# Grouped convolution: semaphores cleared by GpSimd while stores are in flight, store counters taken back by the sync engine's last waits

## The chip, the cores and the metric

One core of one Trainium2 chip. The metric is device time in microseconds (us) of one execution, median over the runs named. "Span" is the stretch that the profile covers, from the first to the last instruction record; the reported time is about 1.7 us longer. SP is the sync engine, which here issues the stores; POOL is GpSimd. Start times and semaphore counts given to a hundredth are from the trace's records.

## The reference

A 3x3 convolution, padded by one, in 8 groups: 16 images of 64 channels of 64x64, 128 output channels, float32 in and out.

```python
for g in range(groups):
    for b in range(batch):
        for co in range(c_out_per_group):
            for ci in range(c_in_per_group):
                for kh in range(k):
                    for kw in range(k):
                        output[b, g * c_out_per_group + co] += \
                            weight[g * c_out_per_group + co, ci, kh, kw] * \
                            x_pad[b, g * c_in_per_group + ci, kh:kh+h, kw:kw+w]
```

## The kernel before

The input is loaded by GpSimd with a cast to bf16, TensorE runs the nine taps as small matmuls, VectorE and ScalarE copy the results from PSUM into 16 output buffers, and SP stores each buffer twice: 32 stores of 1 MiB. Each buffer has its own counter, `st0` to `st15`; a store adds 16 to it when it has landed, so each ends at 32. A small class keeps one counter per engine and drops waits that were already made.

```python
class Order:
    ...
    def wait(self, *needs):
        best = {}
        for need in needs:
            if need is not None:
                sem, val = need
                best[sem.num] = max(best.get(sem.num, (0, sem))[0], val), sem
        for num, (val, sem) in best.items():
            if self.seen.get(num, 0) < val:
                self.eng.wait_ge(sem, val)
                self.seen[num] = val

    def done(self, ins):
        ins.then_inc(self.sem, 1)
        self.n += 1
        return self.sem, self.n
...
    def sem(name):
        s = nc.alloc_semaphore(name)
        sems.append(s)            # everything in sems is cleared at the end
        return s
...
    stored = [sem(f"st{i}") for i in range(NOB)]
...                               # in finish(), once per store
                    SP.wait(*self.wrote[im])
                    nc.sync.dma_start(outf[img][:, s0 : s0 + HALF], ob[slot]).then_inc(stored[slot], 16)
                    uses[slot] += 1
...                               # the end of the program
    SP.wait(*((stored[s], 16 * uses[s]) for s in range(NOB)))
    POOL.wait(SP.done(nc.sync.nop()))
    nc.clear_and_free_semaphores(sems)
```

The compiler packs the 16 last waits into eight SP instructions of two waits each, and puts the signal to GpSimd onto the last of them. Behind this program the tile framework closes the block: all five engines exchange signals, GpSimd clears the framework's own six semaphores, and all are released twice.

## Time and profile before

| | before |
|---|---|
| reported time, median of 6 runs | 130.13 us (129.95 to 130.27) |
| span of the profiled run | 128.2 us |
| last matmul ends | 93.5 us |
| last count of the last store (st15) | 126.81 us |
| from there to the last record (the "tail") | 1.38 us |
| from there to the end of the reported time | 3.09 us |

What bounds the kernel is read in the prediction below. Two more lines of the page of the kernel before, DMA queues with their packets, MB and share of 16 engines, are needed later: queue 1 carries the stores, queue 14 fetches of instructions.

```profile
q1 hardware_dynamic: 4752, 33.59, 62.9%
...
q14 instruction: 2, 0.02, 0.0%
```

From st6 to st15 a store lands every 2.449 us (nine gaps, 22.04 us together before). One MiB in 2.449 us is 428 GB/s, the rate that the view by stretches shows.

### The profile page before, as it was taken

How to read it: one execution, taken by the hardware profiler on the slowest of the kernel's cores; microseconds unless marked ns; L12 is line 12 of the kernel's file. 1: busy time of each engine (PE TensorE's matmuls, PEld its weight loads, DVE VectorE, ACT ScalarE, POOL GpSimd, SP SyncE). 2: the span in 40 equal slices, each digit the busy share in tenths (PEclk: the TensorE clock that was granted, in tenths of full speed). 3: DMA queues.
4: the chain of work that ended last, by engine and by line, in shares of the span. 5: the costliest groups of instructions: out<-in, count | busy, mean ns of one | idle time of the engine just before them, and what ended most of it. 6: DMA issues, size and time to landing. Idle time of an engine off the chain costs nothing.

```text
span 128.2 us, 3808 instructions
## 1 busy us (share of the span) xinstructions
PE 86.9 (68%) x2322; PEld 41.2 (32%) x1170; DVE 45.8 (36%) x74; ACT 37.0 (29%) x68; POOL 7.2 (6%) x19
## 2 busy tenths in 40 slices
PE   0199999999999999999999999999910000000000
PEld 0153353544435355444553544544500000000000
DVE  1840465446444645446544564465440000000000
ACT  4030354345333543336333453354330000000000
POOL 5960000000000000000000000000000000000000
PEclk9999999999999999999999999999996555555555
DMA  2999999999999999999999999999999999999950
GB/s 24 162 202 215 224 212 220 215 289 284 281 289 281 284 271 297 297 401 424 419 424 424 396 435 406 435 414 429 417 424 429 424 432 422 429 427 432 427 243 10
DMA packets 6271, 42.21 MB, mean 329 GB/s; under 512 B 848, under 2 KB 848, under 8 KB 1424
## 3 DMA queue, kind: packets, MB, share of 16 engines
q1 hardware_dynamic: 4752, 33.59, 62.9%
q0 software_dynamic: 1504, 8.39, 32.8%
q8 instruction: 13, 0.21, 0.6%
q14 instruction: 2, 0.02, 0.0%
HBM read 16.81 MB, written 33.55 MB: 393 GB/s over the span
## 4 chain that ended last, share of the span: by engine, by line
PE 67%; DVE 4%; issue 2%; POOL 1%; POOLq 0%; DVEq 0%; SPq 0%
PE bank L227 65%; DVE E L149 2%; DVE ob L254 2%; PE bank L162 2%; POOL ident L128 0%; POOL mask L123 0%; POOL mask L133 0%; POOL xn L106 0%; POOLq L123 0%; POOLq L316 0%; DVEq L75 0%; SPq L53 0%
## 5 line engine op out<-in xcount | busy, mean ns | idle before, releaser
L227 PE MATMUL bank<-xs,wS 32*64 32x504 bf16 (+3 forms) x1152 | 71.6, 374 | 0.6 <-issue 0.4
L227 PE MATMUL bank<-xn,wN 32*64 32x504 bf16 (+3 forms) x1152 | 71.8, 380 | 0.2 <-DVE ob L254 0.2
L254 DVE COPY ob<-bank 128x512 f32<-128x512 f32 x64 | 41.3, 686 | 45.4 <-PE bank L227 45.4
L254 ACT COPY ob<-bank 128x512 f32<-128x512 f32 x64 | 34.5, 589 | 51.2 <-PE bank L227 51.1
L222 PEld LDWEIGHTS <-wS 32*64 32x64 bf16 x576 | 27.5, 104 | 20.8 <-issue 9.9
L222 PEld LDWEIGHTS <-wN 32*64 32x64 bf16 x576 | 19.1, 106 | 25.0 <-issue 20.9
L162 PE MATMUL bank<-ident,E 128*128 128x128 bf16 x18 | 2.1, 313 | 5.9 <-DVE E L149 5.9
L106 POOL DMA_DIRECT2D xs<-in_x_dram x7 | 3.8, 543 | 0.0
L162 PEld LDWEIGHTS bank<-ident,E 128*128 128x128 bf16 x18 | 1.8, 148 | 5.9 <-DVE E L149 5.9
L149 DVE TENSOR_TENSOR E<-w_sb,mask 128x288 bf16<-128x288 f32 x5 | 2.9, 642 | 1.7 <-DMA w_sb<-in_weight_dram 1.7
L106 POOL DMA_DIRECT2D xn<-in_x_dram x5 | 2.9, 583 | 1.0 <-SPq L53 1.0
L172 ACT CAST wS<-bank 128x512 bf16<-128x512 f32 (+1 forms) x3 | 1.2, 487 | 5.2 <-PE bank L162 5.2
L172 DVE CAST wN<-bank 128x512 bf16<-128x512 f32 (+1 forms) x3 | 1.5, 551 | 0.7 <-PE bank L162 0.7
L172 ACT ACT_TABLE_LOAD x1 | 1.3, 1283 | 1.0 <-SPq L53 1.0
L117 DVE MEMSET mask<- 128x8 f32 x1 | 0.1, 65 | 1.1 <-SPq L53 1.1
L128 POOL TENSOR_SCALAR_AFFINE_SELECT ident<-ident 128x128 bf16<-128x128 bf16 x1 | 0.3, 306 | 0.0
L123 POOL TENSOR_SCALAR_AFFINE_SELECT mask<-mask 128x8 f32<-128x8 f32 x1 | 0.2, 211 | 0.1
L133 POOL TENSOR_SCALAR_AFFINE_SELECT mask<-mask 128x8 f32<-128x8 f32 x1 | 0.2, 199 | 0.0
L302 POOL MEMSET const-float32-0.0<- 128x1 f32 x1 | 0.1, 99 | 0.3 <-issue 0.3
L118 DVE MEMSET ident<- 128x64 uint32 x1 | 0.1, 112 | 0.0
L302 POOL MEMSET const-bfloat16-1.0<- 128x1 bf16 x1 | 0.1, 102 | 0.0
L302 POOL MEMSET const-uint8-127<- 128x1 uint8 x1 | 0.1, 102 | 0.0
(1 smaller groups left out, 0.1 us busy)
## 6 DMA issues: line engine op xcount, KB each, us to landing
out_dram<-ob SPq DMA_DIRECT2D x32, 1024.0 KB, 28.0
xn<-in_x_dram POOLq DMA_DIRECT2D x3, 1024.0 KB, 29.6
xs<-in_x_dram POOLq DMA_DIRECT2D x2, 1024.0 KB, 29.6
xn<-in_x_dram POOLq DMA_DIRECT2D x2, 512.0 KB, 7.6
xs<-in_x_dram POOLq DMA_DIRECT2D x2, 512.0 KB, 9.4
xs<-in_x_dram POOLq DMA_DIRECT2D x1, 768.0 KB, 48.4
xs<-in_x_dram POOLq DMA_DIRECT2D x2, 128.0 KB, 9.5
w_sb<-in_weight_dram SPq DMA_DIRECT2D x1, 36.0 KB, 1.8
```

The costliest lines, as they stand in the source:

```text
L106: nc.gpsimd.dma_start(t.rearrange("p h w -> p (h w)")[p0:p1, h0 * W : h1 * W], xr[row0 + p0 : row0 + p1, h0 * W : h1 * W],).then_inc(s, 16)
L117: m1 = DVE.done(nc.vector.memset(mask, 1.0))
L123: m3 = POOL.done(nc.gpsimd.affine_select(out=mask, in_=mask, compare_op=ALU.is_ge, fill=0.0, base=0, channel_multiplier=1, pattern=[[-COg, ...
L128: m4 = POOL.done(nc.gpsimd.affine_select(out=ident, in_=ident, compare_op=ALU.not_equal, fill=1.0, base=0, channel_multiplier=1, pattern=[ ...
L133: m5 = POOL.done(nc.gpsimd.affine_select(out=mask, in_=mask, compare_op=ALU.is_ge, fill=0.0, base=COg - 1, channel_multiplier=-1, pattern= ...
L149: e = DVE.done(nc.vector.tensor_mul(E[:, :, 32 * r : 32 * r + 32].rearrange("p t (g c) -> p t g c", c=CIg), wv.unsqueeze(2).to_broadcast([ ...
L162: ins = nc.tensor.matmul(banks[b][:, 128 * t : 128 * t + 128], E[:, t0 + t, off : off + 128], ident, start=True, stop=True,)
L172: free[b] = eng.done(copy(dst, banks[b][:, 0 : 128 * n]))
L222: pe.ldweights(w_ap, **pos)
L227: ins = pe.add_instruction(mybir.InstMatmult(name=nc.get_next_instruction_name(), engine=mybir.EngineType.PE, start_tensor_calc=k == 0, st ...
L254: free[b] = eng.done(copy(ob[slot][:, o0 : o0 + 512], banks[b]))
L302: nc = _bacc.Bacc("TRN2", target_bir_lowering=False, num_devices=1)
```

## The change

Its intent is to take GpSimd's clear out of the tail. A semaphore may be cleared only when nobody will count on it any more. For all but the store counters that is so when SP has issued its last store, near 100 us. The store counters are therefore left out of GpSimd's list, and each is taken back to zero by the wait that waits for it: "wait until at least 32, then subtract 32".

```diff
-    stored = [sem(f"st{i}") for i in range(NOB)]
+    stored = [nc.alloc_semaphore(f"st{i}") for i in range(NOB)]
...
-    SP.wait(*((stored[s], 16 * uses[s]) for s in range(NOB)))
+
     POOL.wait(SP.done(nc.sync.nop()))
     nc.clear_and_free_semaphores(sems)
+
+    for n in range(nob[0], nob[0] + NOB):
+        s = stored[n % NOB]
+        num = dict(sync_type="semaphore", id=s.num, ant_name=s.name)
+        nc.sync.add_instruction(mybir.InstEventSemaphore(
+            name=nc.get_next_instruction_name(), engine=mybir.EngineType.SP,
+            sync_info=mybir.SyncInfo(
+                on_wait=[mybir.SyncWait(wait_mode="sem-ge-imm", wait_value=16 * uses[n % NOB], **num)],
+                on_update=[mybir.SyncUpdate(update_mode="sem-sub-imm", update_value=16 * uses[n % NOB], **num)],
+            ),
+        ))
```

## The prediction

> **What bounds the kernel now.** I read the page first, for which engine or stage sets the end.
>
> ```profile
> span 128.2 us, 3808 instructions
> PE 86.9 (68%) x2322; PEld 41.2 (32%) x1170; DVE 45.8 (36%) x74; ACT 37.0 (29%) x68; POOL 7.2 (6%) x19
> ...
> PE   0199999999999999999999999999910000000000
> ...
> DMA  2999999999999999999999999999999999999950
> ```
>
> The matrix engine is full for three quarters of the span and idle in the last quarter, while the DMA row stays at 9 until the last two slices. So the last third is a drain of stores. The page's chain of work does not show this: it ends with an eviction at 94.7 us, because it follows engines and not transfers. I therefore asked for busy time by stretches (columns: stretch, length, busy time of each engine, clock, DMA share, GB/s).
>
> ```profile
> 95.00:122.00 27.00, 0.00 (x0) 0.00 (x0) 0.00 (x0) 0.00 (x0) 0.00 (x0) 0.53 1.01 428
> 122.00:126.85 4.85, 0.00 (x0) 0.00 (x0) 0.00 (x0) 0.00 (x0) 0.00 (x0) 0.50 0.35 147
> 126.85:128.20 1.35, 0.00 (x0) 0.00 (x0) 0.00 (x0) 0.00 (x0) 0.00 (x0) 0.50 0.00 0
> ```
>
> For 27 us nothing runs but stores, at 428 GB/s with all DMA engines taken; then the last store trickles out; then 1.35 us pass in which nothing moves at all. The change can touch only those 1.35 us. What fills them stands in the sync engine's waits after 99 us (waiter, releaser, us in total, times, longest):
>
> ```profile
> SPq L75 <- DMA out_dram<-ob: 26.3, 7, 11.9
> SPq L316 <- PEq L316: 0.5, 2, 0.3
> SPq L53 <- POOLq L53: 0.2, 1, 0.2
> ```
>
> and in the view by source line of L285, the clearing call, and of L53, where the tile framework closes the block (operation, count, ns min/median/max, first and last start):
>
> ```profile
> L285 POOLq DRAIN  x1: 116/116/116, 126.9 to 126.9; - x1
> L285 POOLq EVENT_SEMAPHORE_RANGE_CLEAR  x1: 224/224/224, 127.1 to 127.1; - x1
> ...
> L53 SPq NOP  x2: 13/13/13, 0.8 to 127.4; - x2
> ...
> L53 POOLq DRAIN  x1: 40/40/40, 127.4 to 127.4; - x1
> ```
>
> The reader is to see an ordered tail: the last store counted, then GpSimd's drain and clear, then the closing exchange of all five engines, in which the sync engine waits 0.2 us for GpSimd. Start times from the trace's records, in us: the counter of the last store (st15) is full at 126.81; SP passes the wait for it at 126.826, its last wait (st0 and st1, full long before), which also signals GpSimd, at 126.885; GpSimd drain 126.938, clear 127.083, its closing drain 127.356; SP no-op that has waited for that drain 127.422; two SP drains 127.489 and 127.553; GpSimd gathers at 127.585; a second clear and two rounds of release follow, the last record ending at 128.19.
>
> **What the Trainium skill says.** "Perfetto Trace Analysis", section "Sequencer-only Instruction (DRAIN, etc)": the record of such an instruction covers its execution alone; the wait before it and the spreading of its semaphore update after it lie outside. The trace agrees: the waits last 28 ns in the records but follow each other in 59 ns, so I count start to start, not durations. "DMA: Bandwidth & Descriptors", section "Why a DMA increments its semaphore by 16 and not by 1": each of the DMA's engines adds 1 when its own share is written, and only the full 16 means that all has landed. Here st15 gets 15 of its last 16 counts between 122.82 and 125.44 us and the last at 126.81, so one engine is 1.4 us behind, and both kernels must wait for it. "Runtime: NRT & Kernel Launch", section "The ~15µs preamble/postamble breakdown": user semaphores are also zeroed around each launch. The trace shows every semaphore updated once more at 129.0 to 129.28 us, behind the span; the change does not touch that.
>
> **The change part by part.**
>
> Removed from the tail: GpSimd's drain and clear, from 126.938 to the end of the clear at 127.307. In the built program of the changed kernel they wait only for a signal that SP gives behind its last store issue. That issue ran from 99.297 for 0.915 us, so they should run near 100.3 us, in the middle of the store drain, where GpSimd has nothing else to do. The call now covers the semaphores 99 to 116 in place of 99 to 132: 18, not 34. Another clear in this trace covers 6 in 67 ns, so one costs about (224 - 67) / 28 = 5.6 ns, and 18 should take some 135 ns (estimate); off the path it doesn't matter.
>
> Added: the 8 waits of SP on two counters each become 16 waits on one counter each, which also subtract 32. They stand in order of issue, and the counters fill in that order, 2.4 us apart (121.94, 124.38, 126.81 for the last three). At 59 ns each they keep up, and 15 of 16 are done by 124.5 us. Only the last stands on the path, as one did before. A subtraction beside a wait lengthens nothing that I can find: GpSimd's gather in the closing exchange waits and subtracts in a 17 ns record.
>
> Moved: behind the st15 wait came one more SP wait (the pair st0, st1), 59 ns. It is gone.
>
> The new tail: st15's wait at 126.826; the signal that opens the closing exchange came 79 ns behind the last SP wait (126.885 to 126.964), so now at 126.905. Then SP's own steps, by their old spacing: drain +80 ns = 126.985, wait on VectorE and TensorE +74 = 127.059, wait on ScalarE +64 = 127.123, no-op +60 (the usual spacing of SP waits) = 127.183. It no longer waits for GpSimd, whose closing drain comes some 45 ns behind the signal, near 126.95. The no-op moves from 127.422 to 127.183, 0.24 us earlier, and all behind it moves as it is. This agrees with the wait view: 0.21 us of SP waiting for GpSimd, plus the 0.06 us wait removed, less about 0.03 us of issue spacing.
>
> Sum: 0.24 us of 130.17, 0.18%. Predicted: 130.17 - 0.24 = 129.93, say 129.9 us.
>
> **The rivals.**
>
> All of GpSimd's stretch comes back. Its closing drain moves from 127.356 to about 126.95, 0.41 us; if the exchange followed GpSimd alone, the time would be 129.76. Against it: SP's own steps take 0.28 us after the signal whatever GpSimd does, so SP becomes the one that ends the exchange. I give this one chance in six.
>
> The waits take the place of what is removed. Sixteen single waits at 59 ns are 0.94 us against 0.47 for eight pairs. If the last stores landed together, or the first counters last, half of that would be on the path and eat the gain: about 130.2. Against it: stores land in order, 2.4 us apart, because one queue feeds engines that are full. One in twelve.
>
> The clear disturbs the stores. It writes semaphores while 16 DMA engines post increments to others. Should it hold all engines for its whole 135 to 224 ns, the drain would end that much later and the time be 130.1. For it speaks only that the drain is the bound, so nothing there is free; against it, that it writes no counter in use and moves no data. One in twenty. The built program leaves the order of instructions on the other engines as it was, so I see no way for the earlier stages to move; SP has eight waits and one signal more, and they stand ready long before they are due.
>
> The change is lost in the spread. The three runs of before lie 0.24 us apart, 130.03 to 130.27, as much as the gain. The store drain of 31 us needs to move by 1% only to hide it.
>
> **Range and chances.** Mechanisms give 129.76 to 130.2; medians of three runs add about 0.1 us and another chip perhaps 0.2 more. So 129.55 to 130.25 in 8 of 10. A change of over 2% would need 2.6 us, twice all that follows the last store, so faster is near nothing; slower by 2.6 us would need stores slowed by 8%: 1 in 100 each, and 98 of 100 for the same.
>
> **What would show each step right or wrong.** In the profile of the changed kernel: GpSimd's drain and clear of the block near 100.3 us, the clear at 135 ns or so in place of 224; sixteen SP waits, the last one at the filling of the last counter; no wait of SP for GpSimd in the closing exchange; the time from the last count of st15 to the end of the span at 1.14 us in place of 1.38. The stores' rate in 95 to 122 us stays at 428 GB/s and the last count near 126.8 us: that it stays is the weakest step, since it moves by itself from run to run. I'd be wrong if the distance behind the last count did not shrink by 0.15 to 0.35 us, or if the counters filled out of order, or if the store rate fell behind the moment of the clear.

## The result, and the profile after

| | before | changed |
|---|---|---|
| reported time, median of 6 runs | 130.13 us (129.95 to 130.27) | 129.86 us (129.40 to 130.18) |
| ratio | | 0.9976, 95% interval 0.9954 to 0.9999 |
| last count of st15, profiled run | 126.81 us | 126.66 us |
| SP's wait for st15 to SP's no-op | 0.596 us | 0.346 us |
| tail (last count to last record) | 1.38 us | 1.19 us |
| last count to end of reported time | 3.09 us | 2.85 us |

By the 2% measure the time is the same, as predicted, with a gain of 0.27 us between the medians. The page of the changed kernel has the same shape as before:

```profile
span 127.8 us, 3817 instructions
PE 85.8 (67%) x2322; PEld 41.5 (32%) x1170; DVE 45.7 (36%) x74; ACT 37.0 (29%) x68; POOL 7.2 (6%) x19
...
PE   0199999999999999989999999999900000000000
...
DMA  2999999999999999999999999999999999999960
```

Nine instructions more, all on SP; the same full DMA row to the end. The view by stretches of the changed kernel shows the store rate of the drain, 427 against 428 GB/s:

```profile
95.00:122.00 27.00, 0.00 (x0) 0.00 (x0) 0.00 (x0) 0.00 (x0) 0.00 (x0) 0.50 1.01 427
```

The waits of SP after 99 us in the changed kernel:

```profile
SPq L290 <- SPq L290: 26.3, 11, 2.5
SPq L327 <- SPq L327: 0.4, 1, 0.4
SPq L327 <- PEq L327: 0.2, 1, 0.2
```

The line "SPq L53 <- POOLq L53" is gone: SP no longer waits for GpSimd. (Its absence alone would not show this, since the same view of late18, an experiment below, lacks the line too, where the records have SP waiting 0.076 us; that the drain starts at 126.776 us and the no-op at 127.023 does.) The first line's name misleads: L290 seems to wait for itself, because the last update of those counters is SP's own subtraction, but its 11 waits of up to 2.5 us are those for the stores. The views by source line of the clearing call, of the sixteen waits, and of the closing exchange in the changed kernel:

```profile
L285 POOLq DRAIN  x1: 98/98/98, 100.0 to 100.0; - x1
L285 POOLq EVENT_SEMAPHORE_RANGE_CLEAR  x1: 136/136/136, 100.2 to 100.2; - x1
```

```profile
L290 SPq EVENT_SEMAPHORE  x16: 17/17/17, 100.1 to 126.7; - x16
```

```profile
L53 SPq NOP  x2: 13/13/13, 0.8 to 127.0; - x2
...
L53 POOLq DRAIN  x1: 40/40/40, 126.8 to 126.8; - x1
```

The clear runs at 100.2 us in the middle of the drain, in 136 ns. GpSimd's closing drain now comes at 126.8, well ahead of SP's no-op at 127.0; before, it came at 127.4, as the last of the five engines' drains, and the no-op waited for it.

One thing did not fit: the tail shrank by 0.19 us, though SP's no-op moved by 0.25. The very end of the closing exchange is GpSimd's second release and the engines' answers to it. SP's and TensorE's answers (PEld) are these, before and changed:

```profile
L316 SPq EVENT_SEMAPHORE  x2: 17/17/17, 127.7 to 128.1; - x2
...
L316 PEldq EVENT_SEMAPHORE  x2: 51/51/51, 127.7 to 128.1; - x2
```

```profile
L327 SPq EVENT_SEMAPHORE  x2: 17/17/17, 127.3 to 127.8; - x2
...
L327 PEldq EVENT_SEMAPHORE  x2: 51/51/51, 127.3 to 127.7; - x2
```

In the records SP's answer came 0.145 us behind the release, where before it came 0.042 us behind it. TensorE's answer ended the span before, 0.106 us behind the release; SP's ends it now, at 0.162. So SP's lateness of 0.10 us makes the tail only 0.06 us longer, which is what was missing. And 8 KB were fetched on queue 14 right after the span, at 128.48 us, which the trace before did not have.

### The profile page after: what moved, and what is told of

Same layout as the page of the kernel before. It is cut to its first block, busy times and chain, and to the rows that moved or that the text cites. A ratio compares the mean times of both kernels' runs of the same rounds, so it can differ in the third digit from the quotient of the medians.

```text
span 127.8 us, 3817 instructions
## 1 busy us (share of the span) xinstructions
PE 85.8 (67%) x2322; PEld 41.5 (32%) x1170; DVE 45.7 (36%) x74; ACT 37.0 (29%) x68; POOL 7.2 (6%) x19
## 4 chain that ended last, share of the span: by engine, by line
PE 66%; DVE 4%; issue 2%; POOL 1%; POOLq 0%; DVEq 0%; SPq 0%
PE bank L227 64%; DVE E L149 2%; DVE ob L254 2%; PE bank L162 2%; POOL ident L128 0%; POOL mask L123 0%; POOL mask L133 0%; POOL xn L106 0%; POOLq L123 0%; POOLq L327 0%; DVEq L75 0%; SPq L53 0%
## 5 line engine op out<-in xcount | busy, mean ns | idle before, releaser
L227 PE MATMUL bank<-xn,wN 32*64 32x504 bf16 (+3 forms) x1152 | 70.5, 376 | 0.1
L222 PEld LDWEIGHTS <-wS 32*64 32x64 bf16 x576 | 28.0, 104 | 21.1 <-issue 10.2
```

The lines of the kernel that those rows point to most:

```text
L222: pe.ldweights(w_ap, **pos)
L227: ins = pe.add_instruction(mybir.InstMatmult(name=nc.get_next_instruction_name(), engine=mybir.EngineType.PE, start_tensor_calc=k == 0, st ...
```

## The experiments

My theory: the gain is GpSimd's drain and clear leaving the path; SP's own steps then end the exchange. The rivals: the gain is in the waits (fewer on the path, or a shorter clear) and not in the place of the clear; the clear in flight costs the stores something; the difference is store noise. Beside these stood the open question of SP's late last record. Twelve runs were made, all correct. The table gives one profile of each in the measures used, in us; "gap 4-5" is the time between the landings of st4 and st5, in which the early clear falls.

| kernel | wait to no-op | gap 4-5 | last count | tail | last count to end of reported time |
|---|---|---|---|---|---|
| before | 0.596 | 2.451 | 126.81 | 1.38 | 3.09 |
| null | 0.591 | 2.442 | 127.14 | 1.38 | 3.18 |
| bpad9 | 0.588 | 2.451 | 127.04 | 1.43 | 3.10 |
| changed | 0.346 | 2.499 | 126.66 | 1.19 | 2.85 |
| again | 0.345 | 2.509 | 127.03 | 1.19 | 2.86 |
| again2 | 0.346 | 2.499 | 127.08 | 1.19 | 2.85 |
| late18 | 0.481 | 2.471 | 127.23 | 1.32 | 2.98 |
| poolwait | 0.161 | 2.537 | 127.00 | 0.96 | 2.68 |
| poolwait2 | 0.161 | 2.527 | 127.26 | 0.96 | 2.68 |
| reversed | 1.363 | 2.490 | 126.96 | 2.21 | 3.86 |
| clears | 0.345 | 2.649 | 127.41 | 1.19 | 2.84 |
| pad16 | 0.352 | 2.499 | 127.49 | 1.15 | 2.86 |
| pad16b | 0.351 | 2.498 | 127.86 | 1.15 | 2.87 |
| pads340 | 0.346 | 2.480 | 128.12 | 1.14 | 2.86 |

"Wait to no-op" is from SP's (in poolwait GpSimd's) wait for st15 to SP's no-op in the closing exchange. null, again, late18 and poolwait ran on one chip, again2, poolwait2, pad16b and pads340 later on the same one, reversed, clears, bpad9 and pad16 on another.

### The kernel before against itself (null) and the change again (again, again2)

No edit.

> The kernel before against itself, to size the noise. Every theory: ratio 1.000 within some 0.2%, and the stretch from the last count of the last store to the end of the last record (the tail) again 1.38 us, the sync engine's no-op 0.60 us behind its wait for that store. If the tail itself varies by more than 0.05 us, the step-by-step reading of single profiles is not to be trusted.

> The changed kernel again. Theory (GpSimd's drain and clear leave the tail, SP then ends the exchange): tail 1.19 us as in its first profile, no-op 0.35 us behind the wait for the last store, ratio about 0.998. In the first profile SP's very last record came 0.10 us later than in the kernel before, which hid part of the gain; if that belongs to the kernel it shows again (tail 1.19), if it was chance the tail is 1.13 or less. Rival (the change of time is store noise): ratio 1.000 and tails that overlap.

> The changed kernel a third time, for more rounds and as the partner of the next three. Theory: tail 1.19 us; from the last count to the end of the reported time 2.85 us, against 3.09 and 3.18 in the two profiles of the kernel before; ratio near 0.998. If the ratios of its repeats scatter from 0.996 to 1.001, the whole-kernel time cannot show a gain of this size and the tail alone can.

Measured: null 1.0012 (0.9994 to 1.0030); again 0.9998 (0.9977 to 1.0018); again2 0.9977 (0.9960 to 0.9995). With the first comparison's 0.9976 the mean of the three of the changed kernel is 0.9984, about 0.21 us (again and again2 are compared with largely the same runs of the kernel before, and each ratio is good to some 0.2% only). The whole-kernel time barely resolves such a gain; single runs of one kernel differ by 0.8 us (129.58 to 130.38 in again). The tail resolves it in one profile: 1.38, 1.38 before and 1.19, 1.19, 1.19 changed; to the end of the reported time 3.09 and 3.18 against 2.85, 2.86 and 2.85. So store noise is ruled out as the source of that difference, and chance as the reason for SP's late last record (0.134 and 0.145 us again).

### The waits changed, the clear left at the end (late18)

```diff
-    POOL.wait(SP.done(nc.sync.nop()))
-    nc.clear_and_free_semaphores(sems)
     for n in range(nob[0], nob[0] + NOB):
         ...
+    POOL.wait(SP.done(nc.sync.nop()))
+    nc.clear_and_free_semaphores(sems)
```

> Half of the change: the sixteen subtracting waits and the shorter clear of 18 semaphores, but the clear stays behind the waits, in the tail. Theory (the place of the clear is what matters): most of the gain is gone; one SP wait less (0.06 us) but a signal record more, clear 0.09 us shorter, so tail 1.25 to 1.33 us (plus 0.1 if SP's late last record comes with the longer SP program), no-op 0.47 to 0.55 us behind the last wait, ratio about 0.9995. Rival (the shorter clear and the other waits are the gain, the place is not): tail 1.19 or less.

The clearing call in late18, by source line:

```profile
L296 POOLq DRAIN  x1: 98/98/98, 127.3 to 127.3; - x1
L296 POOLq EVENT_SEMAPHORE_RANGE_CLEAR  x1: 138/138/138, 127.5 to 127.5; - x1
```

The no-op comes 0.481 us behind the wait: of the 0.25 us, 0.115 come from the shorter clear and the other waits, 0.135 from the place of the clear. In the records, 0.086 of the 0.115 lie between the start of the clear and GpSimd's closing drain (0.273 us before, 0.187 here). Of the 0.135, 0.059 are SP's signal to GpSimd, which stands behind the last wait here and no longer does in the changed kernel, and 0.076 are SP waiting for GpSimd. The expected 0.47 to 0.55 held, and the tail of 1.32 was within 1.25 to 1.33 even though SP's last record was late here too, for which I had allowed 0.1 more. So both causes are real and about equal; "most of the gain is gone" was too strong. Ratio 0.9993 (0.9972 to 1.0014).

### The waits in reverse order (reversed)

```diff
-    for n in range(nob[0], nob[0] + NOB):
+    for n in reversed(range(nob[0], nob[0] + NOB)):
```

> The changed kernel with the sixteen waits in reverse order, the last store's first. Theory (the waits are free only because they stand in the order in which the stores land): the other fifteen then run behind the last count at 60 to 67 ns each, so the tail grows by 0.9 to 1.0 us to about 2.15 us and the ratio is about 1.005. Rival (a wait that is already satisfied costs nothing): tail stays at 1.19 us.

The waits in reversed, by source line:

```profile
L290 SPq EVENT_SEMAPHORE  x16: 17/17/17, 127.0 to 128.0; - x16
```

The first of the sixteen waits for the last store, and the other fifteen run behind it: 1.02 us, 68 ns each, though each record shows 17 ns. Tail 2.21 us, ratio 1.0049 (1.0009 to 1.0090). A satisfied wait is not free; the sixteen add nothing to the tail in the change because they stand in the order in which the stores land.

(A version with sixteen single waits without subtraction could not be tried: the compiler packs such waits into pairs again, and the built program was the one before.)

### GpSimd takes the waits (poolwait, poolwait2)

```diff
-        nc.sync.add_instruction(mybir.InstEventSemaphore(
-            name=nc.get_next_instruction_name(), engine=mybir.EngineType.SP,
+        nc.gpsimd.add_instruction(mybir.InstEventSemaphore(
+            name=nc.get_next_instruction_name(), engine=mybir.EngineType.Pool,
```

> A further version: as changed, but GpSimd itself takes the sixteen subtracting waits behind its clear, and SP goes on to the closing exchange at once. Theory (after the change SP's own four steps end the exchange): SP has done them near 100 us and waits only for GpSimd's drain, so its no-op comes 0.13 us behind the last wait in place of 0.35; tail 0.97 us, or 0.87 if SP's late last record goes with its shorter program; ratio about 0.996 to 0.997. Rival (the exchange is bound by GpSimd or by the other engines anyway): tail stays at 1.13 to 1.19.

> GpSimd takes the waits, again. Theory: tail 0.96 us, last count to end of the reported time 2.68 us, so 0.41 us better than before and 0.17 better than the change; ratio near 0.997. Rival: as the changed kernel.

SP's waits after 99 us in poolwait, then its lines of the closing exchange:

```profile
SPq L53 <- POOLq L53: 26.5, 1, 26.5
SPq L327 <- PEq L327: 0.5, 2, 0.3
```

```profile
L53 SPq EVENT_SEMAPHORE  x3: 17/27/28, 100.4 to 100.7; - x3
L53 SPq NOP  x2: 13/13/13, 0.8 to 127.2; - x2
```

SP has made its own steps at 100.4 to 100.7 us and stands 26.5 us at the no-op. It comes 0.161 us behind the wait for st15 (0.13 expected; GpSimd's records of this kind follow each other in 95 ns, SP's in 57 to 83), the tail is 0.96 us both times, and 2.68 us to the end of the reported time, 0.17 better than the change. The tail missed what was expected: SP's last record is on time here (0.042 us), for which I had expected 0.87, because I had counted its lateness at 0.10 us of tail and not at the 0.06 told above. The no-op's place confirms that after the change it is SP's own steps that hold it up. In whole time it is not told apart from the change: 0.9987 (0.9967 to 1.0008) and 0.9984 (0.9960 to 1.0008).

### Twenty more clears in flight (clears)

```diff
     nc.clear_and_free_semaphores(sems)
+    for r in range(20):
+        nc.clear_and_free_semaphores([nc.alloc_semaphore(f"x{r}_{k}") for k in range(18)])
```

> The changed kernel with twenty more clears of 18 spare semaphores each by GpSimd behind the first one, while the stores are in flight. Theory (clears in flight disturb nothing): about 20 x 0.25 us = 5 us more of GpSimd records from 100 us on, store rate in that stretch unchanged at 427 to 428 GB/s, time and tail as the changed kernel's, ratio 0.998. Rival (a clear holds up the increments or the stores): if each costs its 0.13 us, the drain ends 2.7 us later, ratio 1.02.

The added clears by source line, and SP's longest wait for a store:

```profile
L287 POOLq EVENT_SEMAPHORE_RANGE_CLEAR  x20: 132/132/134, 100.7 to 106.2; - x20
```

```profile
SPq L292 <- SPq L292: 26.8, 11, 2.7
```

A store came up to 2.7 us after the one before it, where the changed kernel has 2.5. In the records the gaps from st4 to st7, in which the 21 clears fall, are 2.649, 2.720 and 2.542 us, 0.56 us above three times 2.45; the gaps before and far behind are as ever. The three gaps are 0.51 us above the 7.40 us that they take in the changed kernel, so the twenty added calls, each a drain and a clear, hold up the stores by some 25 ns each: my theory that they disturb nothing was wrong, and the rival that each costs its full 0.13 us is out too. The rate over the whole stretch reads 427 GB/s and hides it. Ratio 1.0029 (0.9996 to 1.0062), expected 0.998. The change itself shows the same, but the clear is only half of it. Gap 4-5 is 2.442 to 2.451 in the three profiles of the kernel before (bpad9 among them) and 2.499 to 2.509 in the three of the changed kernel. SP's first five subtracting waits run in this gap too (at 100.1 to 100.4 us in the changed kernel), and two experiments part them. The time from the landing of st4 to that of st6 is, from the records:

| kernels | early clear | subtracting waits in the drain | st4 to st6 |
|---|---|---|---|
| before, null, bpad9 | no | no | 4.889 to 4.899 us |
| late18 | no | yes | 4.926 us |
| reversed | yes | no | 4.928 us |
| changed, again, again2, pad16, pad16b, pads340 | yes | yes | 4.945 to 4.965 us |
| poolwait, poolwait2 (above) | yes | yes, by GpSimd | 4.994 to 5.002 us |

So the clear and the waits cost about 0.03 us each, together 0.05 to 0.07 (0.1 in poolwait, where the other engines' closing steps fall there too), and it is not made up later: from st6 on all of them but pad16 and pad16b run at 2.449 us a store. For each of the two alone there is one profile only.

### SP's program made longer (bpad9, pad16, pad16b, pads340)

```diff
     s_w = sem("w")
     nc.sync.dma_start(w_sb, ...).then_inc(s_w, 16)
+    for _ in range(9):            # 16 in pad16; 200 here and twice 70 between early stores in pads340
+        sp = dict(sync_type="semaphore", id=SP.sem.num, ant_name=SP.sem.name)
+        nc.sync.add_instruction(mybir.InstEventSemaphore(
+            name=nc.get_next_instruction_name(), engine=mybir.EngineType.SP,
+            sync_info=mybir.SyncInfo(
+                on_wait=[mybir.SyncWait(wait_mode="sem-ge-imm", wait_value=SP.n, **sp)],
+                on_update=[mybir.SyncUpdate(update_mode="sem-add-imm", update_value=1, **sp)],
+            ),
+        ))
+        SP.n += 1
```

bpad9 is the kernel before with nine such instructions, the other three are the changed kernel with more.

> The kernel before with nine do-nothing semaphore instructions on SP at its start, so that SP's program is as long as the changed one's. Theory A (the longer SP program makes SP's very last record late by 0.10 us, by where its instruction buffer is refilled): the last SP record now comes 0.14 us behind the last release in place of 0.04, and the tail is 1.45 to 1.48 us. Theory B (chance, or due to the subtracting waits): 0.04 us and 1.38 us.

> The changed kernel with sixteen do-nothing semaphore instructions on SP at its start, where it is idle. Theory A (the place where SP's buffer is refilled): the refill falls among the waits for the stores and is hidden, SP's last record is at 0.04 us behind the last release again, tail 1.13 us, and an 8 KB fetch on queue 14 shows before the end. Theory B (due to the subtracting waits or chance): 0.14 us, tail 1.19.

> Sixteen do-nothing instructions on SP again, which had a tail of 1.15 us but was the slower one, with its last count at 127.49 us. Theory C (the 8 KB instruction fetch for SP, which falls into the store drain at 113 us here and only after the end in the changed kernel, takes 0.3 us of a DMA engine that finishes among the last): last count again at 127.3 to 127.5, ratio about 1.002. Theory D (chance): last count 126.7 to 127.2 as in the other profiles, ratio about 0.998.

> The changed kernel with 340 do-nothing instructions on SP, all in stretches where SP is idle, so that its program takes three 8 KB fetches on queue 14 of its own before the end. Theory C: each costs the last DMA engine 0.3 us, so the last count moves to 127.9 or later and the ratio is about 1.006. Theory D: fetches of this size are lost among the stores, last count 126.7 to 127.2, ratio 0.998 to 1.000.

bpad9 has 80 SP records, as the changed kernel has, and its last one is late (0.140 us behind the release), with a fetch on queue 14 after the span, at 129.26. pad16 has 96, its last record is on time (0.042), and a fetch stands at 113.28 us, between its 80th and 81st record (the waits for st9 and st10). Theory A holds: the late record comes from the length of SP's program, not from the subtractions. The tail of bpad9, 1.43 us, is below the 1.45 to 1.48 expected, for the reason given above: TensorE's answer ends at 0.106 us anyway, so SP's lateness lengthens the tail by 0.05. Nor does it show in the reported time: the last column has 3.10 for bpad9 against 3.09 and 3.18 without it, and 2.86 for pad16 against 2.85. Over all runs the reported time less the span is 1.67 us in the kernels with the late record and 1.73 in the others. The late record makes the span longer, and what follows the span is shorter by about as much.

The surprise is pad16's last count. SP's waits after 99 us in pad16b, and its queue 14:

```profile
SPq L300 <- SPq L300: 26.9, 11, 3.0
```

```profile
q14 instruction: 3, 0.02, 0.0%
```

One store comes 3.0 us after the one before it. In both profiles it is the gap from st9 to st10, 3.010 and 3.028 us in place of 2.45, and that is where the fetch falls (113.28 and 113.64 us). All later gaps are as before, so 0.57 us are lost for good. The packet itself took 0.31 us. Measured ratios: pad16 1.0043 (1.0000 to 1.0086), pad16b 1.0032 (1.0011 to 1.0053), pads340 1.0051 (1.0032 to 1.0070), bpad9 1.0012 (0.9978 to 1.0045). Nine instructions whose fetch falls after the end cost nothing that shows; sixteen, whose fetch falls into the drain, cost 0.57 us in the gap, and the mean of pad16b is 0.69 us above that of again2. Theory C is right in kind: the loss stands twice in the one gap with the fetch. Its size was wrong, 0.57 us and not 0.3, and pad16b's last count of 127.86 lies beyond the 127.3 to 127.5 expected. Other fetches don't confirm it. The last count of pads340, 128.12, and its ratio agree with the theory, but the trace does not tie them to its three fetches, which came at 10.1, 24.5 and 40.0 us: it lags again2 by 0.22 to 0.25 us at the landings from 48 to 64 us, hardly more than again does (0.19 to 0.22), and the rest of its 1.04 us grows between 64 and 77 us. What delays it there stays open. And the fetch in clears (109.66 us, GpSimd's by the lengths of the programs) left no lasting trace in the gaps around it. The latter would fit fetches for different engines falling to different DMA engines, of which only some finish last; the records do not name the DMA engine of a packet, so it is not shown.

## Why the prediction was right

**What bounds the kernel.** Right. Every profile has the same drain at 2.449 us a store, outside the gaps told above, and only the 1.38 us behind the last count, plus what disturbs the drain itself, moved the time.

**The working of the new tail.** Right in its mechanism and nearly in size. Predicted for wait to no-op: 0.36 us in place of 0.60; measured 0.346. Of the terms, the signal came 57 ns behind the wait in place of 79, and the no-op 72 ns behind its predecessor in place of 60; with the steps between them, 11 ns are left over. The clear of 18 semaphores was estimated at 135 ns and took 136. That SP then ends the exchange was shown by poolwait: with SP's steps done early the no-op comes 0.185 us sooner still.

**The tail in the span.** Predicted 1.14 us, measured 1.19. The term missed is SP's last record, late by 0.10 us, and by 0.06 more than TensorE's, since SP's program reaches its 80th record there. I had written that SP's added instructions "stand ready long before they are due"; bpad9 and pad16 show that this is where it failed. It does not reach the reported time.

**The clear in flight.** I gave this rival one chance in twenty, on the ground that it "writes no counter in use and moves no data". It is true in a small way: about 0.03 us for the one clear, 0.51 us for the twenty added. So the step that the change "can touch only those 1.35 us" failed by a little. The gain in the time is therefore about 0.25 us from the tail (the no-op's move) less 0.05 to 0.07 from the drain, 0.2 us, and the mean of the three measured ratios says 0.21.

**The waits in place of what was removed.** Rightly rejected for the tail: they add nothing to it in landing order, and 1.02 us in the other. But a wait with a subtraction takes 66 to 83 ns from start to start, not the 59 of a pair, and the waits cost the drain about 0.03 us, which no rival had.

**Lost in the spread.** Rightly feared. The first comparison (0.27 us) and the first pair of profiles (0.39 us, 129.90 to 129.51) both hold luck: in that pair the last count alone came 0.15 us earlier. The repeats gave 0.9998 and 0.9977. So the agreement of the predicted 129.93 us with 129.86 is partly luck; that of the steps, 0.36 us with 0.346, is not.

**A reading.** Not every semaphore is updated once more behind the span: those of the program are, at 129.01 to 129.28 us, but st15 is not, and others come from 128.9 to 129.5. Nothing rests on it.

The Trainium skill's rule that records of such instructions leave out waiting and spreading ("Perfetto Trace Analysis", "Sequencer-only Instruction (DRAIN, etc)") carried the estimate: fifteen records of 17 ns took 1.02 us in reversed. By durations alone they would have been 0.26.

## What to carry to other kernels

When a kernel ends in a drain of transfers, work that need not wait for the last byte can be moved into the drain, and the engine that makes the last wait should have as few steps as possible behind it: GpSimd making it here gave another 0.17 us, in two profiles and not resolved in the whole time. Waits on many counters add nothing to the tail if they stand in the order in which the counters fill. Measure such a change between two events of one trace, here the last count and the last record, because the whole time scatters by more than the gain; and look past the span too, since SP's late record lengthened the span and not the time. In a drain that is the bound nothing is quite free: a clear of semaphores, subtracting waits and, far more, one 8 KB fetch of instructions came out of the stores' time, so the length of an otherwise idle engine's program can matter.

## What the Trainium skill lacked or had wrong

- No page gives the cost of a clear of a range of semaphores: 67 ns for 6, 132 to 138 for 18, 222 to 225 for 34, so about 33 ns and 5.6 ns for each (worked out from the first and the last).
- No page says that such a clear beside running stores delays them: about 0.03 us for one (reversed), 0.51 us for twenty more in a row, with their drains.
- "Runtime: NRT & Kernel Launch", section "Instruction fetch mechanics", has the refill in blocks of 16 KiB for every engine and its cost as mostly hidden. Here the packets of 16 KB are on queue 8 alone; the refill that follows SP's program (by when it comes in bpad9, pad16 and pads340) is 8 KB on queue 14, and in a store drain one cost 0.57 us of time where its packet took 0.31.
- "Perfetto Trace Analysis", section "Sequencer-only Instruction (DRAIN, etc)", gives no sizes for what lies outside the record: start to start, semaphore instructions that need not wait follow each other in 57 to 83 ns on SP and 95 ns on GpSimd, with records of 17 to 28 ns.
